# The normed input's k tiles laid 2112 bytes apart in SBUF in place of 2048

## The chip, the cores and the metric

The kernel runs on one core of one Trainium2 chip. Its time is the device time of one execution in microseconds. The engines of a core work in parallel, each through its own list of instructions, and wait for each other by semaphores: TensorE (PE) multiplies matrices, VectorE (DVE), ScalarE (ACT) and GpSimd (POOL) do the elementwise work, SyncE (SP) issues transfers. Operands lie in SBUF, a memory of 128 partitions; a tile of `[128, n]` floats takes 4n bytes at the same place in each partition. Products land in PSUM.

## The reference

One block of a network on a sequence of 512 tokens with 1024 channels, all in float32. Two mixers read the same normed input `h`; their sum, gated, goes through an output matrix, and a feed-forward network with 2816 hidden channels follows.

```python
h = rms_norm(x, mix_pre_g[i])
proj = h @ w_in[i]                       # u_glu, z, xbc, dt, gates
...
conv_out = conformer_conv_branch(u_glu, ...)          # GLU, 31-tap depthwise convolution, layer norm, silu, 1024x1024
ssm_out = ssd_branch(z, xbc, dt_raw, ...)             # 4-tap convolution, chunked state space scan, norm, @ ssm_out_w
mixed = (g_conv * conv_out + g_ssm * ssm_out) @ w_out[i]
x = x + rms_norm(mixed, mix_post_g[i])
h = rms_norm(x, ffn_pre_g[i])
gt, up = jnp.split(h @ w_gate_up[i], 2, axis=-1)
f = (jax.nn.silu(gt) * up) @ w_down[i]
x = x + rms_norm(f, ffn_post_g[i])
```

## The kernel before

Every float32 product is made of three products of halves. A matrix is split into an upper half (rounded to the format that PE multiplies at full speed, `F32R`) and a lower half, the rest. `mm3` (L244) issues upper times upper (L246), upper weights times lower input (L248) and lower weights times upper input (L252) into the same PSUM bank. A matmul has two operands in SBUF: the stationary one, a block of 128 x 128 that is loaded into PE beforehand (512 bytes per partition), and the one that is streamed past it, up to 512 columns (2048 bytes). In the profile's names, `px<-hhi,whi` writes `px`, streams `hhi` and has `whi` as the stationary side.

The normed input `h` is kept transposed, channels on the partitions: eight k tiles of 128 channels by 512 tokens. Its upper halves are `hhi`, the lower ones `hlo`; both lie in the pool `hT` at the upper end of SBUF (L275 to L278). `norm_h` (L415) writes them: VectorE multiplies (L420), ScalarE casts to the upper half (L421), VectorE subtracts for the lower (L422). From then on they are read by PE in three ways:

- `proj` (L280) streams a k tile of `hhi` or `hlo` past a block of weights: the projections `pv`, `pg` (GLU, from the fifth on; the first use other tiles, `ehi` and `elo`), `px`, `pB`, `pC` and the gates `pgs`, `pgc`.
- `proj_z0`, `proj_z1` and `proj_zz` want the tokens on the partitions: 128 tokens of a k tile are the stationary side and the weights are streamed, 288, 256 and 512 columns wide. These are the matmuls `pz`.
- Nothing else on PE reads them.

`ssm_out` (L769) multiplies the state space branch's normed output. Its halves `yh` and `yl` are streamed past weights: the matmuls `pso`.

Weights come by DMA in tiles of 1024 floats and are split into `whi` and `wlo` by ScalarE and VectorE (L189 to L212) some tiles ahead of their use. The order of the work around is set by the program: the engines' lists are written in the order of the calls, taps of the depthwise convolution (L514) are put between the matmuls, and a few manual edges (`not_before`) hold an instruction back. The change touches none of it.

Where a tile lies is decided by its pool: tiles of a pool follow each other, and pools are stacked from the lower end, those with `side="right"` from the upper end. The kernel has tiles that are never used and only shift what comes behind them: `place` (160 bytes), `hT_place` (320 bytes), `vT_place` and others. In the built program, the places of PE's operands modulo 512 bytes are:

| tile | streamed or stationary | before | changed |
|---|---|---|---|
| `hhi`, k = 0 ... 7 | both | 160 for every k | 32, 96, 160, 224, 288, 352, 416, 480 |
| `hlo`, every k | both | 160 | 480 |
| `yh`, `yl` | streamed | 160 | 32 |
| weights `whi`, `wlo`, `chi`, `clo` | both | 160 | 160 |
| FFN's first product, input forms (`b11` ... `t4`) | streamed | 352 | 352 |
| FFN's second product, `f_P` ... `f_k` | stationary | 352 | 352 |


Of the kernel before, what the change touches and what calls it, by code (L numbers as in the profile page):

```python
# [10 lines left out]
F32 = mybir.dt.float32  # L11
F32R = mybir.dt.float32r
BF16 = mybir.dt.bfloat16
AF = mybir.ActivationFunctionType
ALU = mybir.AluOpType
# [3 lines left out]
P = 128  # L19
T = 512  # L20
NT = T // P
D = 1024
NK = D // P
DI = 2 * D
H = 32
# [3 lines left out]
GW = DI // G  # L29
# [141 lines left out]
def block_kernel(ctx: ExitStack, tc: tile.TileContext, x, xT, x0, prm, hp, gp, wf, w, out):  # L171
    nc = tc.nc
    act, dve, pe, pool = nc.scalar, nc.vector, nc.tensor, nc.gpsimd
# [39 lines left out]
    def w_split(n, pool_=None, tags=None, bufs=2, parts=1):  # L213
        if n in split or n >= len(ORDER):
            return
        for r in range(n, n + RAW_AHEAD):
            w_raw(r)
        tags, bufs = (tags, bufs) if tags else (("whi", "wlo"), W_BUFS)
        split[n] = [(pool_ or wp).tile([P, 1024], F32R, tag=tg, bufs=bufs, name=f"{tg}_{n}") for tg in tags]
        if parts == 1:  # L220
            w_part(n, slice(0, 1024))

    def w_get(*key, ahead=W_AHEAD):

        n = seq[key]
        for m in range(n, min(n + ahead + 1, seq["pw", 0]) if n < seq["pw", 0] else n + ahead + 1):
            w_split(m)
        return split[n]
# [4 lines left out]
    hlo = None  # L233
# [10 lines left out]
    def mm3(ps, lh, ll, rh, rl, start, stop, more=False, cut=None):  # L244

        mark["pe"] = pe.matmul(ps, lh, rh, start=start, stop=False, skip_group_check=more)  # L246
        if cut is None:
            pe.matmul(ps, lh, rl, start=False, stop=False, skip_group_check=more)  # L248
        else:
            for c in (slice(0, cut), slice(cut, T // 2)):  # L250
                pe.matmul(ps[:, c], lh, rl[:, c], start=False, stop=False, skip_group_check=True)
        mark["pe3"] = pe.matmul(ps, ll, rh, start=False, stop=stop, skip_group_check=more)  # L252
        return mark["pe"]
# [14 lines left out]
    def col(name, i):  # L268
        o = PRM_OFF[name] + i
        return prm_t[:, o : o + 1]  # L270
# [2 lines left out]
    mid = ctx.enter_context(ExitStack())  # L273
    mix = ctx.enter_context(ExitStack())
    hp_pool = mix.enter_context(tc.tile_pool(name="hT", bufs=1, side="right"))  # L275
    hhi = hp_pool.tile([P, NK, T], F32R, tag="hi", name="hhi")
    w3 = hp_pool.tile([P, NK * T], F32, tag="lo", name="w3")
    hp_pool.tile([P, 80], F32, name="hT_place")  # L278

    def proj(ps, wt, rhs=None, ks=slice(0, NK)):  # L280
        wh, wl = wt
        rhi, rlo = rhs or ([hhi[:, k, :] for k in range(NK)], [hlo[:, k, :] for k in range(NK)])
        for k in range(NK)[ks]:
            c = slice(k * P, (k + 1) * P)
            mm3(ps, wh[:, c], wl[:, c], rhi[k], rlo[k], k == 0, k == NK - 1)
# [3 lines left out]
    def va_tile(name):  # L289
        return sp.tile([P, T], F32, tag="va", bufs=VA_BUFS, name=name)  # L290

    def sg_tile(name):
        return sp.tile([P, T], F32, tag="sg", bufs=5, name=name)

    br = ctx.enter_context(ExitStack())
    ssd = br.enter_context(tc.tile_pool(name="ssd", bufs=1))
# [12 lines left out]
    def aux_tile(name):  # L309
        return in_turn("aux", 2, 3, name)  # L310

    def mm_tile(name):
        return in_turn("mm", 5, 3, name)

    def glu_tile(name):
        return in_turn("glu", 5, 5, name)
# [4 lines left out]
    def flat(a):  # L321
        return a.rearrange("p a b -> p (a b)")
# [9 lines left out]
    ps = aux_tile("warm_ps")  # L332
# [11 lines left out]
    for n in range(3):  # L344
        raws[n] = None
        for c in parts.values():
            o = 3 * c.start + n * (c.stop - c.start)
# [67 lines left out]
    def norm_h():  # L415
        nonlocal hlo
        hlo = hp_pool.tile([P, NK, T], F32R, tag="lo", name="hlo")
        for k in range(NK):
            hk = va_tile(f"hk{k}")
            dve.scalar_tensor_tensor(out=hk, in0=xk[k], scalar=col("pre_g", k), in1=rb, op0=ALU.mult, op1=ALU.mult)  # L420
            act.copy(hhi[:, k, :], hk)  # L421
            dve.tensor_tensor(out=hlo[:, k, :], in0=hk, in1=hhi[:, k, :].bitcast(F32), op=ALU.subtract)  # L422


    tri = ssd.tile([P, P], F32, name="tri")
# [2 lines left out]
    dtt = ssd.tile([P, NT, H], F32, name="dtt")  # L428
    nacs = ssd.tile([P, NT, H], F32, name="nacs")
    eacs = ssd.tile([P, NT, H], F32, name="eacs")  # L430
    dec = ssd.tile([P, NT, H], F32, name="dec")
    cd = ssd.tile([P, NT, H], F32, name="cd")
    scr = dr.tile([H, NT, P], F32, name="scr")

# [1 line left out]
    ta, tb, tcx, td, acs, acsT, te = (scratch[:, i, :].rearrange("p (a b) -> p a b", a=NT) for i in range(7))  # L436
# [21 lines left out]
    def running_sums():  # L458
        pcs = aux_tile("pcs")
        pe.matmul(pcs[:, :CH], tri, flat(ta), start=True, stop=True)  # L460
        act.copy(flat(acs), pcs[:, :CH])
        pend = aux_tile("pend")
        pe.matmul(pend[:, :CH], ones, flat(ta), start=True, stop=True)
        act.activation(flat(cd), pend[:, :CH], AF.Exp)
        act.activation(flat(eacs), flat(acs), AF.Exp)
        dve.tensor_tensor(out=flat(tb), in0=pend[:, :CH], in1=flat(acs), op=ALU.subtract)
        act.activation(flat(dec), flat(tb), AF.Exp)
        dve.tensor_scalar(out=flat(nacs), in0=flat(acs), scalar1=-1.0, scalar2=None, op0=ALU.mult)
        pT = aux_tile("pT")
        pe.transpose(pT[:, :P], flat(acs), ident)  # L470
        act.copy(acsT, pT[:, :P])
        for c in range(NT):
            nc.scalar.dma_start(scr[:, c, :], acsT[c * H : (c + 1) * H, :])


    def by_table(ins):

        if "table" in mark:
            not_before(ins, mark["table"])
        mark["table"] = ins  # L480
# [41 lines left out]
    def proj_z0():  # L522

        z = ssd.tile([P, NT, GW], F32, tag="z", bufs=1, name="z0")
        ws = [w_get("zd", j) for j in range(3)]
        for t in range(NT):
            tok = slice(t * P, (t + 1) * P)
            ps = glu_tile(f"pz0_{t}")
            for k in range(NK):
                wh, wl = ws[k // 3]  # L530
                c = slice((k % 3) * (GW + H), (k % 3 + 1) * (GW + H))
                mm3(ps[:, : GW + H], hhi[:, k, tok], hlo[:, k, tok], wh[:, c], wl[:, c], k == 0, k == NK - 1)
            act.activation(z[:, t, :], ps[:, :GW], AF.Silu)
            dve.tensor_tensor(out=ta[:, t, :], in0=ps[:, GW : GW + H], in1=hp_t[:, 0, :], op=ALU.add)
        st[0] = {"z": z}
# [14 lines left out]
    for j in range(NK):  # L550
# [6 lines left out]
        if j == 0:  # L557
            three = [glu_tile(n) for n in ("pv0", "pg0", "pv1")]
            ws = [w_get("val", 0), w_get("glu", 0), w_get("val", 1)]
            for k in range(NK):  # L560
                c = slice(k * P, (k + 1) * P)
# [56 lines left out]
    def proj_z1():  # L618

        z = ssd.tile([P, NT, GW], F32, tag="z", bufs=1, name="z1")  # L620
        ws = [w_get("z", j) for j in range(2)]
        for t2 in range(2):
            ps = mm_tile(f"pz1_{t2}")
            for t in range(2):
                tok = slice((2 * t2 + t) * P, (2 * t2 + t + 1) * P)
                o = ps[:, t * GW : (t + 1) * GW]
                for k in range(NK):
                    wh, wl = ws[k // 4]
                    c = slice((k % 4) * GW, (k % 4 + 1) * GW)
                    mm3(o, hhi[:, k, tok], hlo[:, k, tok], wh[:, c], wl[:, c], k == 0, k == NK - 1)  # L630
            by_table(act.activation(z[:, 2 * t2 : 2 * t2 + 2, :], ps.rearrange("p (a b) -> p a b", a=2), AF.Silu))
        st[1]["z"] = z

    def proj_zz(g):

        z = ssd.tile([P, NT, GW], F32, tag="z", bufs=1, name=f"z{g}")
        zb = [sg_tile(f"zb{g}_{i}").rearrange("p (a b) -> p a b", a=2) for i in range(2)]
        n0 = seq[("zz", 2 * g - 4)]
        w_get("zz", 2 * g - 4, ahead=3)
        st["lo"] = mark["lo"]  # L640
        ws = [w_get("zz", 2 * g - 4 + j, ahead=4 - j) for j in range(4)]
        for t in range(NT):
            tok = slice(t * P, (t + 1) * P)
            ps = mm_tile(f"pz{g}_{t}")
            for k in range(NK):
                wh, wl = ws[k // 2]
                c = slice((k % 2) * T, (k % 2 + 1) * T)
                mm3(ps, hhi[:, k, tok], hlo[:, k, tok], wh[:, c], wl[:, c], k == 0, k == NK - 1)
                if t == NT - 1 and k % 2:
                    w_split(n0 + 5 + k // 2)  # L650
            by_table(act.activation(zb[t // 2][:, t % 2, :], ps[:, :GW], AF.Silu))
            by_table(act.activation(z[:, t, :], ps[:, GW:], AF.Silu))
        st[g]["zb"] = zb
        st.setdefault(g + 1, {})["z"] = z
# [449 lines left out]
    def tm_tiles(key):  # L1104
        return [[bank(f"tm_{key}_{t}_{n}") for n in range(2)] for t in range(NT)]
# [258 lines left out]
    ps = tm_tiles("wo")  # L1364
# [311 lines left out]
    ps = {0: (A[0], C[0]), 2: (A[1], C[1]), 1: (B[0], D_2[0]), 3: (B[1], D_2[1])}  # L1676
# [126 lines left out]
```

## Time and profile before

| | |
|---|---|
| median of 3 runs | 1017.47 us (1017.19 to 1017.85) |
| profiled execution, span from first to last instruction | 1016.0 us |
| PE busy, share of the span | 1007.7 us, 99% |
| PE weight loads busy | 881.7 us, 87% |
| VectorE busy | 847.9 us, 83% |
| ScalarE busy | 616.9 us, 61% |
| granted TensorE clock, mean | 0.998 |

The span is the profiled execution's own time; the runs' median stands 1.5 us above it. A row of the timeline gives the start in us from the span's start, the duration in us, the engine, the line, the operation, its operands and shape. A row of the groups gives line, engine, operation, operands, shape and count, then the busy time in us, the mean of one in ns and the idle time before it. A row of the windows gives the stretch, its length, the busy time (and count) of PE, PE's weight loads, VectorE, ScalarE and GpSimd, the granted clock, the DMA engines' share and GB/s.

### The profile page before, as it was taken

What the parts mean: (1) busy time and instruction counts of PE and PEld (TensorE: products, weight loads), DVE (VectorE), ACT (ScalarE), POOL (GpSimd) and SP (SyncE); (2) the same over time, 40 slices, a digit from 0 to 9 for tenths busy, and PEclk for the clock granted to TensorE, in tenths of its full rate; (3) what the DMA queues carried; (4) which work ended last, traced back from release to release, by engine and by line L of the source; (5) the groups of instructions that cost most, each with busy time, mean ns of one, the idle gap of its engine ahead of it and who ended that gap; (6) DMA issues with size and microseconds to landing.
All of it is one profiled execution on the core that took longest, in us unless ns stands there. A gap on an engine that the chain in (4) does not pass through costs nothing.

```text
span 1016.0 us, 15943 instructions
## 1 busy us (share of the span) xinstructions
PE 1007.7 (99%) x6184; PEld 881.7 (87%) x6184; DVE 847.9 (83%) x1233; ACT 616.9 (61%) x1038; POOL 106.7 (11%) x138
## 2 busy tenths in 40 slices
PE   9999999999999999999999999999999999999997
PEld 7898889888888888888888889889999999998886
DVE  7899977868696879678987889788999887899974
ACT  7655775667666746573552685466666566568552
POOL 0101202120121011100110111012000000001001
PEclk9999999999999999999999999999999999999999
DMA  8567635645554465356452355624755555469622
GB/s 302 151 168 218 158 96 145 187 110 144 158 151 117 130 182 151 102 135 163 99 139 69 114 142 165 223 104 118 230 151 160 153 143 146 128 177 295 212 83 83
DMA packets 43803, 155.02 MB, mean 153 GB/s; under 512 B 5072, under 2 KB 6096, under 8 KB 42704
## 3 DMA queue, kind: packets, MB, share of 16 engines
q1 hardware_dynamic: 30672, 105.44, 30.7%
q0 software_dynamic: 11136, 43.00, 21.7%
q10 hardware_dynamic: 1920, 5.57, 1.6%
q8 instruction: 48, 0.79, 0.3%
q14 instruction: 27, 0.22, 0.1%
HBM read 149.73 MB, written 4.26 MB: 152 GB/s over the span
## 4 chain that ended last, share of the span: by engine, by line
PE 87%; DVE 8%; ACT 3%; issue 1%; DMA 1%; SPq 0%; POOL 0%; POOLq 0%; DVEq 0%; ACTq 0%
PE xy L246 4%; PE xy L252 4%; PE xy L248 4%; PE pso L246 3%; PE pso L248 3%; PE pso L252 3%; PE yv L246 2%; PE yv L252 2%; PE yv L248 2%; PE px L246 2%; PE px L252 2%; PE px L248 2%; DVE a L514 2%; PE pz L248 2%; PE pz L252 2%; PE pz L246 2%
## 5 line engine op out<-in xcount | busy, mean ns | idle before, releaser
L514 DVE SCALAR_TENSOR_TENSOR a<-v,prm_t,a 128x511 f32<-128x511 f32 (+15 forms) x240 | 183.8, 769 | 14.3 <-ACT a L511 12.3
L202 ACT CAST whi<-raw 128x1024 fp32r<-128x1024 f32 x99 | 102.6, 1048 | 127.9 <-PE pso L248 36.7
L209 DVE TENSOR_TENSOR wlo<-raw,whi 128x1024 fp32r<-128x1024 f32 x58 | 70.6, 1220 | 32.7 <-ACT whi L202 32.5
L207 POOL DMA_DIRECT2D wlo<-in_w x41 | 36.5, 891 | 369.1 <-ACT wlo L206 171.4
L248 PE MATMUL pz<-wlo,hhi 128*128 128x512 f32 (+2 forms) x160 | 56.2, 351 | 0.2
L252 PE MATMUL pz<-whi,hlo 128*128 128x512 f32 (+2 forms) x160 | 56.1, 352 | 0.0
L246 PE MATMUL pz<-whi,hhi 128*128 128x512 f32 (+2 forms) x160 | 55.4, 353 | 0.0
L246 PE MATMUL px<-hhi,whi 128*128 128x512 f32 x128 | 50.2, 392 | 0.0
L246 PE MATMUL pso<-yh,whi 128*128 128x512 f32 x128 | 50.2, 394 | 0.0
L252 PE MATMUL px<-hhi,wlo 128*128 128x512 f32 x128 | 49.8, 389 | 0.0
L248 PE MATMUL px<-hlo,whi 128*128 128x512 f32 x128 | 49.8, 389 | 0.0
L248 PE MATMUL pso<-yl,whi 128*128 128x512 f32 x128 | 49.8, 390 | 0.0
L252 PE MATMUL pso<-yh,wlo 128*128 128x512 f32 x128 | 49.7, 390 | 0.0
L1189 ACT CAST whi_g<-raw 128x1024 fp32r<-128x1024 f32 x40 | 41.2, 1052 | 10.6 <-PE yv L248 4.9
L601 DVE SCALAR_TENSOR_TENSOR x<-px,prm_t,x 128x511 f32<-128x511 f32 (+2 forms) x48 | 34.7, 743 | 13.9 <-ACT x L599 13.8
L1196 DVE TENSOR_TENSOR wlo_g<-raw,whi_g 128x1024 fp32r<-128x1024 f32 x34 | 41.3, 1221 | 3.5 <-ACT whi_g L1189 3.4
L206 ACT ACTIVATE wlo<-whi 128x1024 fp32r<-128x1024 f32 x41 | 43.3, 1055 | 0.3
L496 ACT ACTIVATE L<-L,nacs 128x128 f32<-128x128 f32 x128 | 38.8, 389 | 0.1
L248 PEld LDWEIGHTS pz<-wlo,hhi 128*128 128x128 f32 x160 | 30.1, 188 | 4.9 <-DVE wlo L209 1.0
L246 PEld LDWEIGHTS pz<-whi,hhi 128*128 128x128 f32 x160 | 30.2, 189 | 3.9
L252 PEld LDWEIGHTS pz<-whi,hlo 128*128 128x128 f32 x160 | 30.1, 188 | 3.7
L1189 ACT CAST chi_g<-raw 128x1024 fp32r<-128x1024 f32 x24 | 24.9, 1053 | 8.8 <-PE yv L248 3.4
(763 smaller groups left out, 3450.7 us busy)
## 6 DMA issues: line engine op xcount, KB each, us to landing
raw<-in_w SPq DMA_DIRECT2D x182, 512.0 KB, 4.5
wlo<-in_w POOLq DMA_DIRECT2D x41, 512.0 KB, 6.8
L<-scr POOLq DMA_DIRECT2D x8, 1024.0 KB, 7.6
wlo_g<-in_w POOLq DMA_DIRECT2D x11, 512.0 KB, 7.0
clo_g<-in_w POOLq DMA_DIRECT2D x6, 512.0 KB, 5.5
pws<-in_w POOLq DMA_DIRECT2D x8, 256.0 KB, 5.9
pw_raws<-in_w SPq DMA_DIRECT2D x4, 512.0 KB, 7.0
xr<-in_x ACTq DMA_DIRECT2D x4, 512.0 KB, 3.9
```

The source lines that it names most:

```text
L202: mark[n, c.start] = act.copy(hi[:, c], src)
L206: act.activation(lo[:, c], hi[:, c].bitcast(F32), AF.Copy, scale=-1.0)
L207: mark["lo"] = pool.dma_start(lo[:, c], w[n][:, c].bitcast(F32R), accum_op=ALU.add)
L209: mark["wlo"] = dve.tensor_tensor(out=lo[:, c], in0=src, in1=hi[:, c].bitcast(F32), op=ALU.subtract)
L246: mark["pe"] = pe.matmul(ps, lh, rh, start=start, stop=False, skip_group_check=more)
L248: pe.matmul(ps, lh, rl, start=False, stop=False, skip_group_check=more)
L252: mark["pe3"] = pe.matmul(ps, ll, rh, start=False, stop=stop, skip_group_check=more)
L496: act.activation(L[:, h, c, :], L[:, h, c, :], AF.Exp, bias=nacs[:, c, HG * g + h : HG * g + h + 1])
L514: return dve.scalar_tensor_tensor(out=va[j][:, d:], in0=vs[j][:, : T - d], scalar=col("dw_w", j * KC + KC - 1 - d), in1=va[j][:, d:], op0= ...
L601: dve.scalar_tensor_tensor(out=a[:, d:], in0=ps[:, : T - d], scalar=col("ssm_w", i * KS + KS - 1 - d), in1=a[:, d:], op0=ALU.mult, op1=ALU ...
L1189: a_ = act.copy(hi, src)
L1196: d_ = dve.tensor_tensor(out=lo, in0=src, in1=hi.bitcast(F32), op=ALU.subtract)
```

## The change

The k tiles of `hhi` are laid T + 16 floats apart, 2112 bytes in place of 2048, in a tile of 16832 bytes in place of 16384; `hhi` becomes a list of views. The unused tile `hT_place` goes. `hlo`, which takes the place of `w3`, thereby lies 320 bytes higher. The pool grows by 128 bytes; `dec`, of which only three quarters are read, loses its last quarter, 128 bytes, and the tiles behind it, `yh` and `yl` among them, lie 128 bytes lower. The number, kind, shape and order of the instructions stay the same on every engine, but for one exponential, which writes 96 columns of `dec` in place of 128.

```diff
-    hhi = hp_pool.tile([P, NK, T], F32R, tag="hi", name="hhi")
+    HS = T + 16
+    hhi_t = hp_pool.tile([P, NK * HS - 16], F32R, tag="hi", name="hhi")
+    hhi = [hhi_t[:, k * HS : k * HS + T] for k in range(NK)]
     w3 = hp_pool.tile([P, NK * T], F32, tag="lo", name="w3")
-    hp_pool.tile([P, 80], F32, name="hT_place")
...
-        rhi, rlo = rhs or ([hhi[:, k, :] for k in range(NK)], [hlo[:, k, :] for k in range(NK)])
+        rhi, rlo = rhs or (hhi, [hlo[:, k, :] for k in range(NK)])
...
-            act.copy(hhi[:, k, :], hk)
-            dve.tensor_tensor(out=hlo[:, k, :], in0=hk, in1=hhi[:, k, :].bitcast(F32), op=ALU.subtract)
+            act.copy(hhi[k], hk)
+            dve.tensor_tensor(out=hlo[:, k, :], in0=hk, in1=hhi[k].bitcast(F32), op=ALU.subtract)
...
-    dec = ssd.tile([P, NT, H], F32, name="dec")
+    dec = ssd.tile([P, NT - 1, H], F32, name="dec")
...
-        act.activation(flat(dec), flat(tb), AF.Exp)
+        act.activation(dec, tb[:, : NT - 1], AF.Exp)
...
-                mm3(ps, hhi[:, k, tok], hlo[:, k, tok], wh[:, c], wl[:, c], k == 0, k == NK - 1)
+                mm3(ps, hhi[k][:, tok], hlo[:, k, tok], wh[:, c], wl[:, c], k == 0, k == NK - 1)
```

The last pair stands for the same edit in `proj_z0`, `proj_z1` and `proj_zz`.

More of the change, by code (lines that the diff above doesn't have):

```diff
@@ L531, in proj_z0 @@
                 c = slice((k % 3) * (GW + H), (k % 3 + 1) * (GW + H))
-                mm3(ps[:, : GW + H], hhi[:, k, tok], hlo[:, k, tok], wh[:, c], wl[:, c], k == 0, k == NK - 1)
+                mm3(ps[:, : GW + H], hhi[k][:, tok], hlo[:, k, tok], wh[:, c], wl[:, c], k == 0, k == NK - 1)
             act.activation(z[:, t, :], ps[:, :GW], AF.Silu)
@@ L629, in proj_z1 @@
                     c = slice((k % 4) * GW, (k % 4 + 1) * GW)
-                    mm3(o, hhi[:, k, tok], hlo[:, k, tok], wh[:, c], wl[:, c], k == 0, k == NK - 1)
+                    mm3(o, hhi[k][:, tok], hlo[:, k, tok], wh[:, c], wl[:, c], k == 0, k == NK - 1)
             by_table(act.activation(z[:, 2 * t2 : 2 * t2 + 2, :], ps.rearrange("p (a b) -> p a b", a=2), AF.Silu))
```

## The prediction

> **What bounds the kernel now.** I read the profile's page first, then the list of waits of TensorE, then the timeline of single matmuls in four stretches.
>
> ```profile
> span 1016.0 us, 15943 instructions
> PE 1007.7 (99%) x6184; PEld 881.7 (87%) x6184; DVE 847.9 (83%) x1233; ACT 616.9 (61%) x1038; POOL 106.7 (11%) x138
> PE 87%; DVE 8%; ACT 3%; issue 1%; DMA 1%; SPq 0%; POOL 0%; POOLq 0%; DVEq 0%; ACTq 0%
> ...
> PE warm_ps L334 <- DVE woken L329: 1.0, 1, 1.0
> PE pxT L667 <- DVE yl L763: 0.4, 1, 0.4
> ...
> 300.00:400.00 100.00, 100.00 (x577) 83.33 (x577) 77.89 (x110) 61.77 (x116) 14.45 (x16) 1.00 0.53 139
> ```
>
> TensorE (PE) is busy for 99% of the span, 87% of the chain that ended last is matmuls, and its two longest waits are 1.0 and 0.4 us. The last row is 100 us in the middle of the mixers: PE 100.00 us busy, weight loads 83.33, VectorE 77.89, ScalarE 61.77, clock 1.00. The only way for this kernel to become faster or slower by microseconds is that a matmul takes another time, or that PE waits. The 11% of the chain on VectorE and ScalarE say that a gain of PE may be lost by about that share; a loss is not hidden.
>
> A matmul's record overlaps the next one's, so its price is the distance between two starts:
>
> ```profile
> 110.18 0.39 PE L246 MATMUL px<-hhi,whi 128*128 128x512 f32 x1
> 110.41 0.39 PE L248 MATMUL px<-hlo,whi 128*128 128x512 f32 x1
> ...
> 111.54 0.39 PE L246 MATMUL px<-hhi,whi 128*128 128x512 f32 x1
> ...
> 110.18 0.19 PEld L248 LDWEIGHTS px<-hlo,whi 128*128 128x128 f32 x1
> ```
>
> The two L246 rows are six matmuls apart: 1.36 / 6 = 226.7 ns each. The PEld row is the weight load of the second matmul; it starts at 110.18, with the first one, and ends after 0.19 us: under each matmul the stationary block of the next is loaded. So two reads of SBUF run at a time, the streamed tile and the next stationary block. I call "distance" the place of the streamed tile less the place of the block that is loaded under it, modulo 512 bytes. Above, all places are 160: distance 0.
>
> **The change part by part.** The built program has the same instructions in the same order on every engine. Nothing is added or removed, no DMA and no wait; what differs is places (table above) and two smaller things at the end of this part. The matmuls that see another distance, from the page's groups and the lines of the same three forms:
>
> ```profile
> L246 PE MATMUL px<-hhi,whi 128*128 128x512 f32 x128 | 50.2, 392 | 0.0
> L246 PE MATMUL pso<-yh,whi 128*128 128x512 f32 x128 | 50.2, 394 | 0.0
> L246 PE MATMUL pgs<-hhi,whi 128*128 128x512 f32 x64 | 25.8, 403 | 0.0
> L246 PE MATMUL pB<-hhi,whi 128*128 128x512 f32 x64 | 25.6, 401 | 0.0
> L246 PE MATMUL pC<-hhi,whi 128*128 128x512 f32 x64 | 25.6, 401 | 0.0
> L246 PE MATMUL pgc<-hhi,whi 128*128 128x512 f32 x64 | 25.4, 397 | 0.0
> L246 PE MATMUL pv<-hhi,whi 128*128 128x512 f32 x32 | 12.6, 395 | 0.0
> L246 PE MATMUL pg<-hhi,whi 128*128 128x512 f32 x32 | 12.4, 389 | 0.0
> L246 PE MATMUL pz<-whi,hhi 128*128 128x512 f32 x96 | 36.8, 393 | 0.0
> ```
>
> Each of these groups comes three times (L246, L248, L252). The projections that stream h: 128 + 4 x 64 + 2 x 32 = 448 times three; of these 896 stream an upper half and 448 a lower half. The output product streams y: 128 x 3 = 384. The gate z streams weights and loads h as the stationary side: 96 x 3 = 288 of 512 columns, and by the program 96 of 256 (z1) and 96 of 288 (z0). New distances: upper halves 384 + 64k, that is 384, 448, 0, 64, 128, 192, 256, 320; lower halves 480 - 160 = 320; y 32 - 160 = 384; in z 160 - 480 = 192 where a lower half is loaded, and the same eight values as above where an upper half is.
>
> What a distance costs, from the stretches that have another one:
>
> ```profile
> 162.94 0.28 PE L246 MATMUL pz<-whi,hhi 128*128 128x256 f32 x1
> ...
> 163.66 0.28 PE L246 MATMUL pz<-whi,hhi 128*128 128x256 f32 x1
> ...
> 799.89 0.28 PE L246 MATMUL xy<-t2h,whi_g 128*128 128x256 f32 x1
> ...
> 800.57 0.28 PE L246 MATMUL yv<-b22h,chi_g 128*128 128x256 f32 x1
> ...
> 960.17 0.39 PE L246 MATMUL tm_d<-chi_g,f_Q 128*128 128x512 f32 x1
> ...
> 967.73 0.39 PE L246 MATMUL tm_c<-whi_g,f_q 128*128 128x512 f32 x1
> ...
> 54.36 0.30 PE L246 MATMUL pz<-whi,hhi 128*128 128x288 f32 x1
> ...
> 60.73 0.29 PE L246 MATMUL pz<-whi,hhi 128*128 128x288 f32 x1
> ```
>
> First pair, z1, distance 0, 256 columns, 6 matmuls: 0.72 / 6 = 120.0 ns. With 226.7 for 512 columns, 256 more columns cost 106.7, so a matmul is its columns (213.3, 120.0 and 106.7 ns for 512, 288 and 256) and an extra of 13.3 ns at distance 0. Second pair, the FFN's first product, streamed at 352 and loaded at 160, distance 192, 6 matmuls: 0.68 / 6 = 113.3, extra 6.7. Third pair, the FFN's second product, streamed at 160 and loaded at 352, distance 320, 33 matmuls: 7.56 / 33 = 229.1, extra 15.8. Fourth pair, z0, 48 matmuls whose streamed slices lie at 160, 288 and 416, distances 0, 128 and 256 by turns: 6.37 / 48 = 132.7, extra 12.7. The same shape costs 120.0 and 113.3 at two distances, so the distance matters, by up to 15.8 - 6.7 = 9.1 ns. I take an extra to belong to the distance alone.
>
> Distances 64, 384 and 448 stand in no row. Bounds are the cheapest and the dearest row, 6.7 and 15.8; none of the rows is nearer to them than the others, so I take the middle, 11.2.
>
> - Upper halves, 896: mean extra (13.3 + 12.7 + 12.7 + 6.7 + 15.8 + 3 x 11.2) / 8 = 11.9, against 13.3: -1.4 x 896 = -1.3 us.
> - Lower halves, 448 at distance 320: +2.5 x 448 = +1.1 us.
> - y, 384 at distance 384: -2.1 x 384 = -0.8 us.
> - z with 512 columns: 96 at 192, -6.6 x 96 = -0.6 us; 192 over the eight distances, -1.4 x 192 = -0.3 us. z1: 32 at 192 and 64 over the eight, -0.2 - 0.1 = -0.3 us. z0 was already mixed and stays so: 0, with both ends at 96 x 6 ns = 0.6 us.
>
> Sum -2.2 us. With the unknown distances at their ends, 336 + 384 + 72 + 24 = 816 matmuls move by 4.6 ns each, 3.7 us: from -5.9 to +1.5 us.
>
> The rest: the exponential that makes `dec` covers 96 columns in place of 128, once.
>
> ```profile
> L467 ACT ACTIVATE dec<-scratch x1: 305/305/305, 90.3 to 90.3; 128x128 f32<-128x128 f32 x1
> ```
>
> It is a part of 0.3 us on ScalarE, 61.77 us busy of 100 above; cost nothing, and below 0.3 us without that cover. ScalarE's casts and VectorE's subtractions that write the halves move the same contiguous rows to other places; no row shows a price of that, and there are 8 of each: nothing.
>
> The profiled execution's span is 1016.0 us, the median of the runs 1017.47, so 1.5 us lie around the span. 1016.0 - 2.2 = 1013.8 for the span, 1015.3 for the runs.
>
> **The rivals.** *It never settles* (slower). After a break PE takes a while to come back to its pace:
>
> ```profile
> 87.93 0.40 PE L248 MATMUL pv<-hlo,whi 128*128 128x512 f32 x1
> ...
> 90.01 0.39 PE L248 MATMUL pv<-hlo,whi 128*128 128x512 f32 x1
> ...
> 91.37 0.39 PE L248 MATMUL pv<-hlo,whi 128*128 128x512 f32 x1
> ```
>
> The nine matmuls from 87.93 took 2.08 us, 231.1 each, the six after them 226.7, at the same distance 0. So the pace is a state that repetition reaches, and a kernel whose distance changes from one matmul to the next may never reach it. At 231.1 the 1344 + 288 matmuls that use h cost 4.4 x 1632 = +7.2 us, and y at the dearest uniform row +2.5 x 384 = +1.0: 1025.7 us. It decides as soon as a group of 24 (eight k, three products) averages over 228 ns. Against it: z0 has such a mixture and its extra, 12.7, is below the settled 13.3.
>
> *Few distances are dear* (faster by more). If only 0 and 320 are dear and the other six cost 6.7 as 192 does, upper halves have (13.3 + 15.8 + 6 x 6.7) / 8 = 8.7: -4.1 us; lower halves +1.1; y -2.5; z -0.6 - 0.9 - 0.5: together -7.5, 1010.0 us. z0's 12.7 over 0, 128 and 256 speaks against it, but the unknown 64, 384 and 448 might do part of it.
>
> *Places do not matter* (the change does nothing to the time). Then 120.0 against 113.3 would come from something else in which the two stages differ, and 1017.5 us stays. The Trainium skill, in "TensorE: Matmul & The Clock Gate", section "Step-by-step: what each phase is for", has a rule for this: "Loading the next tile's weights doesn't steal SBUF read bandwidth from the running matmul." By that rule this rival holds; the trace disagrees as far as the two 256-wide rows can tell.
>
> **How the numbers follow.** Forecast 0.46, never settles 0.25, few are dear 0.18, no matter 0.11. A change under 0.2%, 2.0 us, cannot be told from none here. The forecast's own range, 1011.5 to 1019, holds faster 0.25, same 0.18, slower 0.03. With the others: faster 0.25 + 0.18 = 0.43, same 0.18 + 0.11 = 0.29, slower 0.03 + 0.25 = 0.28. The range goes from 1009 to 1023: all of the forecast, most of the fast rival, and the slow rival where it holds for two thirds of its matmuls.
>
> **What would show it.** In the changed kernel's timeline 24 matmuls of a projection should take 16 x 225.2 + 8 x 229.1 = 5436 ns, as now, but unevenly: those that stream a lower half some 4 ns longer than the mean of those with an upper half; the shortest starts at k = 5; the output product 224.5 each; z with 512 columns 223.6. The FFN rows, 113.3 and 229.1, must not move, and PE must stay at 99% without new waits. The forecast is wrong if the extra doesn't follow the distance: if the 24 take over 5.47 us with no k cheaper than another, the state decides; if all stay at 226.7, places don't matter.

## The result and the profile after

The changed kernel took 1024.77 us (median of 4 runs, 1024.43 to 1025.20) against 1017.43 us (1017.19 to 1017.85) for the kernel before: a ratio of 1.0072 (95% interval 1.0058 to 1.0086). It is slower by 7.3 us, where 2.2 us of gain were forecast.

The profile's page of the changed kernel: the span, the engines' busy time, and the chain that ended last by engine.

```profile
span 1023.0 us, 15943 instructions
PE 1015.2 (99%) x6184; PEld 882.2 (86%) x6184; DVE 845.5 (83%) x1233; ACT 617.2 (60%) x1038; POOL 107.1 (10%) x138
...
PE 96%; DVE 2%; ACT 1%; DMA 1%; SPq 0%; issue 0%; POOLq 0%; DVEq 0%; POOL 0%; ACTq 0%
```

The span grew by 7.0 us and PE's busy time by 7.5, with the same 6184 matmuls; VectorE (847.9 us before) and ScalarE (616.9) hardly differ. PE's own list of waits has nothing new; the wait for `yl` (0.4 us) is no longer in it:

```profile
PE warm_ps L335 <- DVE woken L330: 1.0, 1, 1.0
PE xy L246 <- DVE f L1397: 0.2, 1, 0.2
```

So the matmuls themselves became longer. Where, the lists of one tile's instructions show (line, operands, count, duration in ns as least/median/most, first and last start in us). Before:

```profile
L246 PE MATMUL px<-hhi,whi x128: 389/389/578, 108.1 to 439.4; 128*128 128x512 f32 x128
...
L246 PE MATMUL pso<-yh,whi x128: 387/389/578, 241.9 to 543.4; 128*128 128x512 f32 x128
...
L246 PE MATMUL pgc<-hhi,whi x64: 387/389/799, 554.9 to 600.5; 128*128 128x512 f32 x64
...
L246 PE MATMUL tm_c<-whi_g,fh_q x8: 389/389/389, 968.4 to 1006.1; 128*128 128x512 f32 x8
```

Changed:

```profile
L246 PE MATMUL px<-hhi,whi x128: 388/395/588, 108.6 to 443.6; 128*128 128x512 f32 x128
...
L246 PE MATMUL pso<-yh,whi x128: 390/393/583, 243.3 to 549.3; 128*128 128x512 f32 x128
...
L246 PE MATMUL pgc<-hhi,whi x64: 388/395/794, 561.2 to 607.6; 128*128 128x512 f32 x64
...
L246 PE MATMUL tm_c<-whi_g,fh_q x8: 389/389/390, 975.4 to 1013.1; 128*128 128x512 f32 x8
```

The first `px` starts 0.5 us later than before, the last 4.2, the last `pso` 5.9, the last gate matmul 7.1; the last product of the FFN is still 7.0 us late. The whole loss arises where h and y are read, and nothing is lost or won back after it.

The price of one matmul is again the time between two starts. Starts stand in the rows to 0.01 us, so a mean over 45 matmuls is good to 0.2 ns and one over 6 to 2 ns. The changed kernel's timeline: the first unit of `px` from its first to its last L246 matmul (45 matmuls apart), the output product (33 apart), z1 (24 apart), and a stretch of the FFN's first product (6 apart):

```profile
108.62 0.40 PE L246 MATMUL px<-hhi,whi 128*128 128x512 f32 x1
...
119.04 0.40 PE L246 MATMUL px<-hhi,whi 128*128 128x512 f32 x1
...
243.29 0.40 PE L246 MATMUL pso<-yh,whi 128*128 128x512 f32 x1
...
250.95 0.40 PE L246 MATMUL pso<-yh,whi 128*128 128x512 f32 x1
...
163.24 0.28 PE L246 MATMUL pz<-whi,hhi 128*128 128x256 f32 x1
...
166.04 0.28 PE L246 MATMUL pz<-whi,hhi 128*128 128x256 f32 x1
...
806.93 0.28 PE L246 MATMUL xy<-t2h,whi_g 128*128 128x256 f32 x1
...
807.61 0.28 PE L246 MATMUL yv<-b22h,chi_g 128*128 128x256 f32 x1
```

The same stretch of the output product before:

```profile
241.91 0.39 PE L246 MATMUL pso<-yh,whi 128*128 128x512 f32 x1
...
249.39 0.39 PE L246 MATMUL pso<-yh,whi 128*128 128x512 f32 x1
```

10.42 / 45 = 231.6 ns for the projections (226.7 before), 7.66 / 33 = 232.1 for y (7.48 / 33 = 226.7 before), 2.80 / 24 = 116.7 for z1 (120.0 before: the one thing that became cheaper), 0.68 / 6 = 113.3 in the FFN, as before. Below, "h", "y", "z" and "z1" stand for the mean step from one start to the next over all such matmuls in a trace (columns alone take 213.3 ns for 512 and 106.7 for 256; steps more than 30 ns above that, which stand at breaks, are left out): the projections, the output product, the gate z with 512 columns, and with 256.

| | h | y | z | z1 |
|---|---|---|---|---|
| before, ns | 227.4 | 227.1 | 227.4 | 119.7 |
| changed, ns | 231.9 | 232.3 | 231.3 | 116.8 |
| matmuls by the program | 1344 | 384 | 288 | 96 |
| difference, us | +6.0 | +2.0 | +1.1 | -0.3 |

Together +8.9 us. Summed as they are, with the steps at breaks, the same matmuls take 7.5 us longer, so breaks give 1.4 us back: some of PE's waits for other engines, like the one for `yl`, became shorter. PE's share of the chain grew from 87% to 96% and VectorE's fell from 8% to 2%. So part of a loss is hidden after all. PE's other matmuls up to the gates' end give back 0.4, which leaves the 7.1 us by which the last gate matmul is late.

One thing stands in the changed kernel's timeline already. These are the steps in ns, worked out from single starts, of the first 24 matmuls of `px` (k = 0 to 7, three products each, one k between bars):

```
233 231 231 | 229 233 235 | 225 232 233 | 232 232 234
233 231 231 | 229 233 235 | 225 233 232 | 232 233 233
```

The second row repeats the first to 1 ns. k and k + 4 lie 256 bytes apart. By the prediction's prices distances 0 and 256, or 64 and 320, had nothing to do with each other.

### The profile page after: what moved, and what is told of

The parts are those of the page before. It is cut to its first block, busy times and chain, and to the rows that moved or that the text cites. A ratio compares the mean times of both kernels' runs of the same rounds, so it can differ in the third digit from the quotient of the medians.

```text
span 1023.0 us, 15943 instructions
## 1 busy us (share of the span) xinstructions
PE 1015.2 (99%) x6184; PEld 882.2 (86%) x6184; DVE 845.5 (83%) x1233; ACT 617.2 (60%) x1038; POOL 107.1 (10%) x138
## 4 chain that ended last, share of the span: by engine, by line
PE 96%; DVE 2%; ACT 1%; DMA 1%; SPq 0%; issue 0%; POOLq 0%; DVEq 0%; POOL 0%; ACTq 0%
PE xy L246 4%; PE xy L252 4%; PE xy L248 4%; PE pz L252 3%; PE pz L246 3%; PE pz L248 3%; PE pso L246 3%; PE px L248 3%; PE pso L248 3%; PE pso L252 3%; PE px L246 3%; PE px L252 3%; PE yv L248 2%; PE yv L252 2%; PE yv L246 2%; PE yd L710 2%
## 5 line engine op out<-in xcount | busy, mean ns | idle before, releaser
L515 DVE SCALAR_TENSOR_TENSOR a<-v,prm_t,a 128x511 f32<-128x511 f32 (+15 forms) x240 | 180.8, 756 | 15.6 <-ACT a L512 13.6
L246 PE MATMUL pz<-whi,hhi 128*128 128x512 f32 (+2 forms) x160 | 55.7, 355 | 0.0
L246 PE MATMUL pso<-yh,whi 128*128 128x512 f32 x128 | 50.8, 400 | 0.0
L246 PE MATMUL px<-hhi,whi 128*128 128x512 f32 x128 | 50.8, 397 | 0.0
L246 PEld LDWEIGHTS pz<-whi,hhi 128*128 128x128 f32 x160 | 30.1, 188 | 4.1
```

Source lines behind the costliest of these rows:

```text
L515: return dve.scalar_tensor_tensor(out=va[j][:, d:], in0=vs[j][:, : T - d], scalar=col("dw_w", j * KC + KC - 1 - d), in1=va[j][:, d:], op0= ...
```

## The experiments

Three accounts had to be told apart. **Prices**: each distance has a price of its own, the forecast only had wrong ones. **Never settles**: the prediction's rival, every mixture of distances runs at some 231 ns, whatever the distances. **Columns**: the price belongs to the distance and the width of the streamed tile together, so that 6.7 ns for 256 columns says nothing on 512.

The expectations use names of their own: theories S and M say that a change of distance costs by itself, D and U that each distance has a price and no more.

Each experiment's time is a single one. The kernel before took 1019.6, 1016.8, 1018.2 and 1016.9 us on the four occasions, so single times are good to 2 or 3 us, and each is set against the kernel before of its own occasion; what a place costs is read from steps in the trace, which repeat within 0.1 ns where nothing changes (FFN's second kind of product, `yv`: 113.33 to 113.35 in every run but the one that moves it). The granted clock was 0.998 to 1.000 in all of these runs. Where room is needed, or y would move, three small tables (`eacs`, `dec`, `cd`) lose 512 bytes that nobody reads, as the change does with `dec`; this edit isn't repeated in the diffs.

### The two halves of the change

y alone (`y_only`): distance 384 for y, h as before.

```diff
-    dec = ssd.tile([P, NT, H], F32, name="dec")
+    dec = ssd.tile([P, NT - 1, H], F32, name="dec")
-        act.activation(flat(dec), flat(tb), AF.Exp)
+        act.activation(dec, tb[:, : NT - 1], AF.Exp)
```

> The kernel before with one part of the change alone: dec without its last quarter, so that y's halves lie at 32 in place of 160 (distance 384 in all of their 384 matmuls). Theory S (a matmul settles when the same distance repeats, and the change spoils the repetition): y repeats one distance, so it settles at 225 to 229 ns each, at most +0.9 us. Theory D (each distance has its own price, and 0 is a cheap one): 232.3 ns each as in the changed kernel against 227.0, +2.0 us, about 1019.5 us.

```profile
242.32 0.40 PE L246 MATMUL pso<-yh,whi 128*128 128x512 f32 x1
...
250.01 0.39 PE L246 MATMUL pso<-yh,whi 128*128 128x512 f32 x1
```

7.69 / 33 = 233.0 ns; h, z and z1 as before (227.4, 227.2, 119.7). 1020.12 us against 1019.6: the time alone can't tell, the steps say +6.0 x 384 = 2.3 us. Every y matmul sees the same distance here, so nothing mixes: 384 is dear by itself, as theory D has it. The forecast had y cheaper, by 0.8 us.

h alone (`h_only`): the change's places of `hhi` and `hlo`, y left at distance 0.

```diff
-    hhi = hp_pool.tile([P, NK, T], F32R, tag="hi", name="hhi")
+    HS = T + 16
+    hhi_t = hp_pool.tile([P, NK * HS - 16], F32R, tag="hi", name="hhi")
+    hhi = [hhi_t[:, k * HS : k * HS + T] for k in range(NK)]
-    hp_pool.tile([P, 80], F32, name="hT_place")
```

> The changed kernel's places for h (32 + 64k and 480), with y's halves back at 160; the room comes from unread parts of dec, cd and eacs. If the two parts add, h 231.9, z with 512 columns 231.3 and y 227.1 ns: the changed kernel's loss less y's, 7.3 - 2.0 = +5.3 us. If y's place alone disturbed h, h would fall below 230.

h 231.8, z 231.5, z1 116.8, as with the whole change; y 227.9 (226.7 in its settled stretches). 1022.93 us against 1018.19. The steps of h, z and z1 are those of the whole change: by the steps, y's place and h's hardly touch each other. The times, 4.7 us here, 0.5 in `y_only` and 7.3 with both, are single ones and can't decide it.

Upper halves alone (`hhi_only`): the pitch as above, `hT_place` kept, so upper halves at distance 64 + 64k and lower halves at 0.

> The upper halves alone at a pitch of 2112 bytes (places 224 + 64k), lower halves and y's halves back at 160; the room comes from unread parts of dec, cd and eacs. Theory S: every matmul that uses h still sees another distance than the one before it, so all 1344 + 288 stay at 231 to 232 ns: +6.5 us, about 1024. Theory D: only the 896 with an upper half (and two thirds of z) pay, some 231.9 against 227.3, the 448 with a lower half are back at 227: +4.5 us, about 1022.

```profile
109.10 0.40 PE L246 MATMUL px<-hhi,whi 128*128 128x512 f32 x1
...
119.57 0.40 PE L246 MATMUL px<-hhi,whi 128*128 128x512 f32 x1
```

10.47 / 45 = 232.7 ns, h over the kernel 232.6, z 231.5; 1024.56 us against 1019.6. The lower halves, still at distance 0, took 232.2 each, not 227.3 as before: a matmul pays for what its neighbours do. That speaks for the rival, and against any account by prices alone.

### One distance for all of h

The unused tile behind `w3` moves both halves of h together, so a projection sees one distance and nothing mixes. The size is 80 floats for distance 0; 0, 16, 32, 48, 64, 72 floats give 320, 256, 192, 128, 64, 32.

```diff
-    hp_pool.tile([P, 80], F32, name="hT_place")
+    hp_pool.tile([P, 32], F32, name="hT_place")
```

That is `u192`; in `u320` the line goes. y moves along or by a tile of its own ahead of it (`y_place`).

> One pitch of 2048 bytes, everything at one place again, but at 480 in place of 160: h's halves and y's halves at distance 320 in every matmul that streams them, 192 where z loads h. Theory S: they settle at the FFN's 229.1 (1728 x 2.4 = +4.1 us), z with 512 columns at 220.0 (-1.9) and with 256 at 113.3 (-0.6): about 1019. Theory D: 232.4 as the lower halves cost in the changed kernel (1728 x 5.5 = +9.5 us), z 230.2 (+0.8): about 1028.

> As the run with one place for all, at 352: h and y at distance 192 in every matmul that streams them, 320 where z loads h. Theory S: they settle at the extra of the FFN's first product, 213.3 + 6.7 = 220.0 ns (1728 x -6.7 = -11.6 us), z at 229.1 (+0.7): about 1006.5. Theory D with the changed kernel's prices at 192 (230.3 and 235.3): 1728 x 5.9 = +10.2 us, z +0.9: about 1028.5.

The first unit of `px`, 45 matmuls, in the timeline of `u320`; behind it z1, whose distance there is 160 - 480 = 192, over 21 matmuls:

```profile
109.05 0.39 PE L246 MATMUL px<-hhi,whi 128*128 128x512 f32 x1
...
119.34 0.39 PE L246 MATMUL px<-hhi,whi 128*128 128x512 f32 x1
...
164.10 0.28 PE L246 MATMUL pz<-whi,hhi 128*128 128x256 f32 x1
...
166.48 0.28 PE L246 MATMUL pz<-whi,hhi 128*128 128x256 f32 x1
```

The same unit of `px` in `u192`; behind it a stretch of z with 512 columns, whose distance there is 160 - 352 = 320, over 15 matmuls:

```profile
109.25 0.39 PE L246 MATMUL px<-hhi,whi 128*128 128x512 f32 x1
...
119.75 0.39 PE L246 MATMUL px<-hhi,whi 128*128 128x512 f32 x1
...
207.53 0.39 PE L246 MATMUL pz<-whi,hhi 128*128 128x512 f32 x1
...
210.96 0.39 PE L246 MATMUL pz<-whi,hhi 128*128 128x512 f32 x1
```

At 320, 10.29 / 45 = 228.7 ns, as the FFN's second product says. At 192, 10.50 / 45 = 233.3 ns: the extra is 20.0, where 256 columns in the FFN have 6.7. z confirms both with the roles exchanged: at 320 3.43 / 15 = 228.7 (h streamed at 320: the same), and at 192, in `u320`, 233.3 over the kernel. And z1 in `u320`, 256 columns at 192, takes 2.38 / 21 = 113.3, the FFN's price, where it took 120.0 at 0. So it is not the stage: 192 is the cheapest distance for 256 columns and one of the dearest for 512. **Columns** holds. Of the expectations, S held at 320 (229.1) and missed 192 by 13 ns (220.0); D the other way round (232.4 at 320, and 227.3 + 5.9 = 233.2 at 192). Times: 1021.65 and 1026.94 us against 1019.6; the second run loses 7.3 us, as much as the change, without any mixture, which **never settles** alone can't give.

> One distance for all of h, 64 (448 where z loads h), y at 352. If theory U is right the eight distances' prices must average to the 232 ns that the upper halves cost in the changed kernel; with 226.7, 228.9, 233.3 and 233.3 measured for 0, 320, 192 and 384, the four of 64, 128, 256 and 448 must then average 233.5 or more. Under M they may lie anywhere between 220 and 233.

> One distance for all of h, 128 (384 where z loads h, which must come out at 233.3 as y alone did), y at 160. Under U 128 costs 233 or more, +8 us for h; under M it may settle lower.

> One distance for all of h and z, 256, y at 224. Under U 256 costs 233 or more, +8 us for h and +1.7 for z; under M it may settle lower. If any of these places costs less than 226.7, it is a better place than the kernel has.

The same unit of `px`, 45 matmuls, in the timelines of `u64`, `u128` and `u256`, in this order:

```profile
108.12 0.39 PE L246 MATMUL px<-hhi,whi 128*128 128x512 f32 x1
...
118.42 0.39 PE L246 MATMUL px<-hhi,whi 128*128 128x512 f32 x1
```

```profile
109.28 0.40 PE L246 MATMUL px<-hhi,whi 128*128 128x512 f32 x1
...
119.79 0.39 PE L246 MATMUL px<-hhi,whi 128*128 128x512 f32 x1
```

```profile
108.06 0.39 PE L246 MATMUL px<-hhi,whi 128*128 128x512 f32 x1
...
118.26 0.39 PE L246 MATMUL px<-hhi,whi 128*128 128x512 f32 x1
```

10.30 / 45 = 228.9 at 64, 10.51 / 45 = 233.6 at 128, 10.20 / 45 = 226.7 at 256. So 64 costs what 320 does, 128 what 384 does in `y_only`, 256 what 0 does; and z in `u64`, at 448, has 233.3, as at 192. The price repeats every 256 bytes. The four that U wanted at 233.5 or more (64, 128, 256, 448) average (228.9 + 233.6 + 226.7 + 233.3) / 4 = 230.6, so prices alone don't give the changed kernel's upper halves. y was put at other distances in these three: 352 (that is 96) 233.5, 160 234.1, 224 233.3, as means over the kernel. Times 1022.34, 1027.76 and 1019.84 us against 1016.83; `u256` pays for y alone (6.2 x 384 = 2.4 us).

At 128 the price is not a single one. In the first unit of `px` in `u128` the steps go 238, 229 and over again, 233.4 in the mean; in other stretches of the same trace they go 232, 231, 232, 228, 230, 233, 241 and over again, 232.4. `y_only`, at 384, has the first pattern in its early stretches and the second from 526 us on, and y in the changed kernel has the second throughout. So at one and the same distance PE can settle in two ways, 1 ns apart; no run shows what chooses between them.

The finer step (`fine_32`): h and y at distance 32, and the FFN's input forms 32 bytes higher, so its first product is at 224 and its second at 288.

```diff
-MOV_AT = 192
+MOV_AT = 224
-    hp_pool.tile([P, 80], F32, name="hT_place")
+    hp_pool.tile([P, 72], F32, name="hT_place")
```

> One distance of 32 for h and y (480, that is 224 modulo 256, where z loads h), and the FFN's input forms at 384 in place of 352 (distance 224 in its first product, 288 or 32 modulo 256 in its second). Under a period of 256 bytes the runs so far have 512 columns at 0: 226.7, 64: 228.9, 96: 233.5, 128: 233, 160: 234.1, 192 and 224: 233.3. 32 is the one left: between 226.7 and 229 if the price rises steadily from 0 to 64, below 226.7 if the best place lies beside 0. The FFN's first product at 224 costs more than the 113.3 of 192 if 192 is its best place.

```profile
109.17 0.40 PE L246 MATMUL px<-hhi,whi 128*128 128x512 f32 x1
...
119.67 0.39 PE L246 MATMUL px<-hhi,whi 128*128 128x512 f32 x1
...
701.27 0.28 PE L246 MATMUL xy<-b11h,a01h 128*128 128x256 f32 x1
...
703.39 0.28 PE L246 MATMUL xy<-b11h,a01h 128*128 128x256 f32 x1
```

233.3 ns for h at 32, and 2.12 / 18 = 117.8 for the FFN's 256 columns at 224 (118.3 over the kernel, 113.3 at 192). 1038.08 us against 1018.19: 20 us from shifts of 32 bytes, most of it in h (7.9 us by the steps) and in the FFN's two kinds of 256-wide products (5.3 and 3.2). Both readings that the expectation named for 32, between 226.7 and 229 or below 226.7, missed. The FFN's second product, which streams weights past its input forms and has 512 columns, came from 320 to 288, that is 32, and went from 228.9 to 233.2: the price of 32 stands with the roles exchanged too.

### Two distances, far and near in this period

`mix_0_320` and `mix_0_256` leave every upper half at distance 0 and put the lower halves at 320 and at 256; both mix two distances at every matmul.

```diff
     hhi = hp_pool.tile([P, NK, T], F32R, tag="hi", name="hhi")
+    hp_pool.tile([P, 80], F32, name="h_gap")
     w3 = hp_pool.tile([P, NK * T], F32, tag="lo", name="w3")
-    hp_pool.tile([P, 80], F32, name="hT_place")
```

In the second the gap is 64 floats and `hT_place` has 16.

> The fewest distances that can alternate: every upper half at 160 (distance 0), every lower half at 480 (distance 320), pitch 2048; y at distance 256. Repeated alone, 0 costs 226.7 ns and 320 costs 228.9. Theory U (a matmul costs what its distance costs when repeated): the mean of h's matmuls is (2 x 226.7 + 228.9) / 3 = 227.4, +0.1 to +1.0 us over the 1344. Theory M (alternation itself costs, whatever the distances): 230 to 232 ns, +4 to +6 us. y at 256 stands apart: its mean gives the price of 256.

```profile
109.00 0.39 PE L246 MATMUL px<-hhi,whi 128*128 128x512 f32 x1
...
119.44 0.39 PE L246 MATMUL px<-hhi,whi 128*128 128x512 f32 x1
```

> Upper halves at 160, lower halves at 416 (distances 0 and 256 by turns), y at 160, all else as in the kernel before. The run with one distance of 256 everywhere gave h 227.4 ns, the price of distance 0. Theory M256 (what alternates is the distance modulo 256, and 0 and 256 are the same): h stays at 227.4 and the time at that of before, within 1 us. Theory M512 (any alternation of places costs, as 0 and 320 by turns cost 231.9): h at 231 to 232, +6 us.

```profile
107.24 0.39 PE L246 MATMUL px<-hhi,whi 128*128 128x512 f32 x1
...
117.44 0.39 PE L246 MATMUL px<-hhi,whi 128*128 128x512 f32 x1
```

10.44 / 45 = 232.0 ns with 320, 226.7 with 256. Two matmuls of three at 226.7 and one at 228.9 would be 227.4: the mixture itself costs 4.6 ns, and it costs nothing where both places are the same modulo 256. 1023.34 us against 1016.83, and 1016.52 against 1018.19; the second has the steps of the kernel before in every stage (h 227.4, y 227.1, z 227.6, z1 119.7), so its 1.7 us are not put down to it. The steps of `mix_0_320`, 15 to a row:

```
230 237 241 224 226 229 233 232 231 236 231 229 233 235 233
230 237 241 224 226 229 233 232 231 236 231 229 233 235 233
230 237 241 224 226 229 233 232 231 236 231 229 233 235 233
```

The program repeats every 3 matmuls, the steps every 15. The same matmul form costs 230, 224, 233, 236 and 233 by turns: a step depends on what the steps before it left, and not on its distance alone.

How long that lasts, `half_64` asks: k = 0 to 3 at a distance of 0 modulo 256, k = 4 to 7 at 64, both halves, so that the distance changes once in 12 matmuls.

```diff
+    HW = NK * T + 16
+    at_k = [k * T + 16 * (k // 4) for k in range(NK)]
...
+    hhi = [hhi_t[:, a : a + T] for a in at_k]
+    hp_pool.tile([P, 48], F32, name="h_gap")
...
+        hlo = [hlo_t[:, a : a + T] for a in at_k]
```

> All halves of k = 0 to 3 at a distance that is 0 modulo 256 bytes, all halves of k = 4 to 7 at one that is 64 modulo 256; y stays at 0. So the distance changes only after every twelve matmuls of a projection, not at every matmul. Prices add up: h at (226.7 + 228.9) / 2 = 227.8 ns, with z at (227.4 + 233.3) / 2 = 230.3 the span is 1016.0 + 1344 x 1.1 ns + 288 x 3 ns = 1018.3 us. Each change of distance costs a few matmuls at the unsettled pace (nine after a break, at 231 ns): h between 229 and 230.5, span 1020 to 1022. Any mixture, however seldom it changes, costs as much as the one at every matmul (231.9): span 1023.

```profile
108.27 0.40 PE L246 MATMUL px<-hhi,whi 128*128 128x512 f32 x1
...
118.65 0.39 PE L246 MATMUL px<-hhi,whi 128*128 128x512 f32 x1
```

10.38 / 45 = 230.7 ns, h over the kernel 230.4 (z 231.0, z1 118.4, y 227.8), 1021.25 us against 1016.91, a span of 1019.5: the middle account, a few matmuls at the unsettled pace after each change (h within the 229 to 230.5 named for it, the span just under its 1020). The steps of one unit:

```
234 231 233 236 224 231 236 228 233 231 226 227
237 235 231 232 226 229 232 226 229 231 226 229
```

The second row is in the pattern of `u64` (226, 229, 232) from the fifth step on and costs 2763 ns, 16 above 12 x 228.9; the first comes near 226.7 only at its end, 2770 ns, 50 above 12 x 226.7. From its third step on it has the steps of the stretch after a break that the prediction showed from 87.93 us on: in the kernel before these go 233 236 224 231 236 228 232 231 227 and then stay at 226 and 227. So PE comes to distance 0 from 64 by the same steps as from a break. Twelve matmuls are too few to settle at distance 0.

## Why the prediction was wrong

**What bounds the kernel**: right. PE is the bound, the loss is in PE's steps, and neither the exponential, the casts, DMAs nor a wait shows a part in it. "A loss is not hidden" was wrong by 1.4 us.

**The failed step is "I take an extra to belong to the distance alone"**, and with it the bounds of 6.7 and 15.8 ns. It fell in two ways.

First, it carried prices from 256 to 512 columns. The runs' prices for one distance throughout, in ns, distances modulo 256:

| distance | 0 | 32 | 64 | 96 | 128 | 160 | 192 | 224 |
|---|---|---|---|---|---|---|---|---|
| 512 columns | 226.7 | 233.3 | 228.9 | 233.5 | 233.6 | 234.1 | 233.3 | 233.3 |
| 256 columns | 120.0 | | 117.6 | | 118.6 | | 113.3 | 118.3 |

(117.6 and 118.6 are z1 in `u192` and `u128`; 96, 160 and 224 with 512 columns are y's means over the kernel; 128 can also settle at 232.4.) For 512 columns distance 0, where the kernel was, is the cheapest of all, by 2.2 ns at least; nothing that the change did to h, y and z could gain. The middle of 11.2 that I took for 64, 384 and 448 is really 15.6, 20.3 and 20.0, 192, put at 6.7, is 20.0, and 128, put at 12.7 after the mixed z0, is 20.3. With these prices the same sum comes out on the other side:

| term | forecast | by uniform prices | measured |
|---|---|---|---|
| upper halves, 896 | -1.3 | +3.6 | |
| lower halves, 448 | +1.1 | +1.0 | |
| both | -0.2 | +4.6 | +6.0 |
| y, 384 | -0.8 | +2.7 | +2.0 |
| z, 288 | -0.9 | +1.4 | +1.1 |
| z1, 96 | -0.3 | -0.4 | -0.3 |

Only the lower halves' term, which stood on a row with 512 columns, and z1, which is the 256-wide one, were priced right. Upper halves: two distances each at 0, 64, 128 and 192, extras 13.3, 15.6, 20.3 and 20.0, mean 17.3, so +4.0 x 896; lower halves +2.3 x 448; y +7.0 x 384; z +6.7 x 96 and +4.0 x 192; z1 likewise from the lower row of the prices. y came out below its +2.7 since it settled at 232.4 and not at 233.6; at that price it is +2.2.

Second, the sum of single prices leaves out that a change of distance costs by itself. By prices h would have taken (16 x 230.6 + 8 x 228.9) / 24 = 230.0 ns; the first unit of `px` took 231.6. In `mix_0_320` that part stands alone, 232.0 against 227.4.

**"It never settles"** gave 1025.7 us for a measured 1024.77, at 231.1 ns for h and z where 231.9 and 231.3 were measured. Its size was right, its mechanism is part of the truth: of the 4.9 ns by which the first unit of `px` grew (226.7 to 231.6), 3.3 are dear distances, as `u192` and `u128` pay them with no mixture, and 1.6 the changes of distance. So part of its good number is luck: it priced one state for every mixture, where `mix_0_256` mixes at no cost and `u192` pays without mixing. What I held against it, z0 with its mixture and an extra of 12.7, was a weak test: two of z0's three distances, 0 and 256, are the same, its width is 288, and no row has that width at one distance.

**"Few distances are dear"** is the reverse of what holds for 512 columns: all but 0 and 64 are. **"Places do not matter"** fell with `u256` against `u128`: the same program but for the size of unused tiles, 226.7 against 233.6 ns. The rule of the Trainium skill that was weighed there ("TensorE: Matmul & The Clock Gate", section "Step-by-step: what each phase is for": "Loading the next tile's weights doesn't steal SBUF read bandwidth from the running matmul") doesn't agree with these runs, as far as the weight load is what the streamed tile meets. That the second of the two is the block loaded under it, is supported by the exchange of roles (h streamed at 320 and z at 320 cost the same, likewise at 192), but in every run that gives a price the block being loaded and the one in use lie at the same place modulo 256, so no run tells one from the other. What inside the chip has a phase of 256 bytes stays open.

**What the prediction named as signs**: the 24 matmuls took 231.6 x 24 = 5558 ns, over the 5.47 us named; k = 5 was not the shortest, the L246 matmuls of k = 2 and 6 were (225 and 225 above), which are 0 and 256; those that stream a lower half stood 0.9 ns above the mean of the others, not 4. The FFN and PE's 99% stayed, as said.

A better kernel than the one before is within reach only by little: moving the FFN's second product from 320 to 0 would give 2.2 ns in each of its matmuls at that distance (348 in the trace, 0.8 us), z1 at 192 another 0.6 us. Both together stay under the 2.0 us that can be told from nothing, and they were not tried.

## What to carry to other kernels

When matmuls run back to back, each with a new stationary block, check the places of the streamed tile and of the stationary block modulo 256 bytes; here shifts of 32 bytes in unused tiles cost 2%. Put them for the widest products first, and give all tiles of a loop one place modulo 256, since alternating costs by itself, 4.6 ns of 227.4 here. A price taken from one shape is not a price for another: it takes a run with the same width, and one with the same sequence.

## What was not expected of the hardware

- The step at 512 columns depends on places with a period of 256 bytes: 226.7 ns at 0, 228.9 at 64, 232.4 to 234.1 at the six others measured.
- The order of prices turns around with the width: 192 is the cheapest at 256 columns (113.3 against 120.0 at 0) and dear at 512.
- One distance can settle in two ways: at 128 modulo 256 a pattern of two steps, 233.4 in the mean, and one of seven, 232.4, stand in one trace (`u128`, and `y_only` too).
- Settled steps are not always equal: at distance 64 they go 226, 229, 232 and over again; `mix_0_320` needs 15 steps to repeat where its program needs 3. After a change of distance it takes from 4 to more than 10 matmuls to settle.
